# Strassen-Winograd output projections: the second product by halves in turn with the first two, and one weight sum by accumulating DMA

## The chip, the cores and the metric

The kernel runs on one core of one Trainium2 chip, in float32. The metric is the device time of one execution in microseconds (us). TensorE (PE) multiplies; PEld is its weight load, which runs beside the multiplication. VectorE (DVE), ScalarE (ACT) and GpSimd (POOL) do the rest; SyncE (SP) and POOL issue DMA transfers between HBM and the on-chip memory (SBUF). TensorE writes into PSUM, of which this kernel uses eight banks.

## The reference

One layer of a decoder trunk with 512 tokens and 1024 channels (cut to what matters here):

```python
def reference(x, mem, ...):
    h = rmsnorm(x, norm_mix_g)
    proj = h @ w_in                                  # three branches and their gates
    up = einsum('bsnw,nwd->bsnd', branches, w_branch)
    merged = sum(sigmoid(gate_logits + b_gate) * up, axis=2)
    x = x + merged @ w_o                             # output projection 1
    h = rmsnorm(x, norm_xa_g)
    mem_n = rmsnorm(mem, norm_mem_g)
    x = x + memory_attention(h, mem_n, w_xq, w_xkv, w_xo)   # ends with o @ w_xo: projection 2
    h = rmsnorm(x, norm_mlp_g)
    x = x + square(relu(h @ w_up)) @ w_down
    return rmsnorm(x, final_g)
```

The two projections `merged @ w_o` and `o @ w_xo` are 512 x 1024 by 1024 x 1024 each; the sum with `x` is normalized right behind each of them.

## The kernel before, in words

**Precision.** Every float32 operand is split into a high and a low half (`fp32r`), and a product is three matmuls: high by high, high by low, low by high. For weights this is `parts_of` (lines 104 to 114): ACT casts the high half out of the raw block (line 112), VectorE subtracts it from the raw block (line 113). Both halves go into `w_part` buffers; there are ten (`WBUFS`), so five blocks are in flight. Raw blocks (`w_raw`, 128 x 1024, 512 KB) have six buffers (`RAWS`) and are loaded by SP in the order of a `Stream` (line 241).

**Seven products.** The projections with `w_o`, `w_xo` and `w_down` go by Strassen and Winograd: `items_w` (line 410). The 512 tokens are two halves of 256 (rows of A), the output channels two halves of 512 (columns of B), and seven products P1 to P7 take the place of eight. `LEFT` (line 405) names the left operand of each; these are made by `Pairs` (lines 376 to 403) for two blocks of 128 channels at a time, into `pr` tiles, and A12, which only P2 reads, into `pr_b`. The right operands are B11 (P1), B21 (P2), B22 (P3) and sums of blocks (P4 to P7). `TO` (line 407) says where each product's bank is added: P1 and P2 to the left 512 columns of tokens 0 to 255, P6 and P3 to the right columns of these, P5 and P7 to the right columns of tokens 256 to 511, P4 to their left ones. P1, P6, P7 and P4 accumulate in the two banks p1, P5 and P3 in the two banks p3, both from the pool `at`; P2 has two banks p2 from the pool `mm`, which has four and serves the ordinary projections. The add into `x` reads a bank in the middle of its use, so P6 waits for the adds of P1, and P3 for those of P5.

**Halves.** The inner dimension of a product comes in two halves, j = 0 and 1, each a raw block for each of B11, B12, B22 and B21: eight blocks of a set, in the load order B11 (j = 0), B12 (0), B11 (1), B12 (1), B22 (0), B22 (1), B21 (0), B21 (1). One half of a product is 12 matmuls of 128 x 512 (line 430). `ORDER` (line 177) is the order in which the halves are written: P1 and P5 by halves in turn, then P6, P3, P2, P7, P4 with both halves together.

**Weight sums.** Class `Wide` makes the sums on VectorE in place in the raw blocks (lines 191 to 200, `plus` in line 131): B11 + B12 for P5, two sums for P6, B11 + B21 for P4, each for both halves: eight sums of a set. `w_o` and `w_down` use it. Class `Summed` (lines 202 to 221), for `w_xo`, makes the same sums by accumulating DMAs from HBM that POOL issues (line 213).

**Norms.** `proj_norm` (line 1035) hangs work on the ends of the products: after P3 it loads the gain through POOL and begins the norm of tokens 0 to 255 with the sum of squares over the right columns (`norm_begin`, line 494); after P2 `norm_end` (line 503) takes the left columns, the power on POOL (line 480) and the scaled `xn`; after P7 it begins tokens 256 to 511 and transposes the first tile; after P4 it ends those. Beside the first projection the norm of the memory is made (`mem_norm`) and transposed after P6 and P3 through banks of the pool `at` into `mT_h` and `mT_l`, which the projection of the keys reads right after P4. Between the first and second item of the second projection stand the last two heads of the attention (`last_heads`, line 1166), whose results are left operands of the second halves.

**What sets the order.** The code calls the steps in the order of a list (`plan`, `run_plan` in line 266), and `Stream.pump` makes the weights' parts two steps ahead. That is not yet the order on the chip: the context of line 1369 plans the instructions of every engine with its own model of their durations, takes from what is ready the earliest of the list, and gives out buffers and banks as they come free. Each engine's order is then fixed in the program, and an engine waits for the instruction at its head.

Of the kernel before, what the change touches and what calls it, by code (L numbers as in the profile page):

```python
# [38 lines left out]
def trunk_kernel(ctx: ExitStack, tc: tile.TileContext, x, mem, par, rot, dqd, kdec, g_mix, g_xa, g_mem, g_mlp,  # L39
# [64 lines left out]
    def parts_of(src):  # L104
        n = src.shape[1]
        part = lambda: wpool.tile([P, CW], F32R, name="w_part", bufs=WBUFS)
        if 2 * n <= CW:
            both = part()
            wh, wl = both[:, :n], both[:, n:2 * n]
        else:  # L110
            wh, wl = part(), part()
        act.copy(out=wh, in_=src)  # L112
        dve.tensor_tensor(out=wl, in0=src, in1=wh.bitcast(F32), op=ALU.subtract)  # L113
        return wh, wl
# [28 lines left out]
    class Seven:  # L143
# [27 lines left out]
        def get(self):  # L171
            where = dict(B11=(0, 0), T1=(1, 0), T3=(1, 1), T2=(2, 0), T4=(2, 1), B22=(3, 0), B21=(3, 1))
            return {n: [w[:, o * 512:(o + 1) * 512].rearrange("p (a b) -> p a b", a=4) for w in self.parts[i]]
                    for n, (i, o) in where.items()}


    ORDER = [(p, j) for pair in (("P1", "P5"), ("P6",), ("P3",), ("P2",), ("P7",), ("P4",)) for j in (0, 1) for p in pair]

    class Wide:

        def __init__(self, t, c):
            self.t, self.c = t, c
            self.loads = [(t, c + i) for i in range(8)]
            at = dict(P1=0, P5=1, P6=4, P3=4, P2=6, P7=6, P4=6)
            self.need = [at[p] + (2 * j if at[p] < 4 else j) + 1 for p, j in ORDER]
            self.steps = [lambda raw, p=p, j=j: self.step(raw, p, j) for p, j in ORDER]
            self.parts = []

        def step(self, raw, p, j):
            b11, b12, b22, b21 = (raw[i] if i < len(raw) else None for i in (2 * j, 2 * j + 1, 4 + j, 6 + j))
            if p == "P5":
                plus(b11, b11, b12)
            elif p == "P6":
                plus(b11, b11, b22)
                plus(b12, b12, b22)
            elif p == "P4":
                plus(b11, b11, b21)
            return parts_of(dict(P3=b22, P2=b21, P7=b12).get(p, b11))  # L200

    class Summed(Wide):


        def __init__(self, t, c):
            super().__init__(t, c)
            self.need = [n + (n in (1, 3)) for n in self.need]

        def step(self, raw, p, j):
            b11, b12, b22, b21 = (raw[i] if i < len(raw) else None for i in (2 * j, 2 * j + 1, 4 + j, 6 + j))  # L210

            def acc(dst, i):
                pool.dma_start(out=dst, in_=self.t[self.c + i], accum_op=ALU.add)

            parts = parts_of(dict(P3=b22, P2=b21, P7=b12).get(p, b11))
            if p == "P1":
                acc(b11, 2 * j + 1)
                acc(b12, 4 + j)
            elif p in ("P5", "P6"):
                acc(b11, 4 + j if p == "P5" else 6 + j)  # L220
            return parts

    class Stream:
# [186 lines left out]
    def items_w(src, c, pairs, after=lambda p: None, kind=Wide):  # L410


        acc = {}

        def part(p, js, n):
            bank = dict(P2="p2", P5="p3", P3="p3").get(p, "p1")

            def fn(ws):
                ws = [wv(w, 2) for w in ws]
                if p in ("P1", "P5", "P2") and js[0] == 0:  # L420
                    for i in range(2):
                        acc[bank, i] = (mmps if p == "P2" else atps)(bank)

                def mm(i, j):
                    tok = slice(i * P, (i + 1) * P)
                    for k in range(2):
                        ah, al = [x[:, tok] for x in pairs(2 * j + k)[LEFT[p]]]
                        wh, wl = [w[:, k, :] for w in ws[j - js[0]]]
                        for m, (x, y) in enumerate(((ah, wh), (ah, wl), (al, wh))):
                            te.matmul(acc[bank, i], x, y, start=p in ("P1", "P5", "P2") and j + k + m == 0,  # L430
                                      stop=j == 1 and k == 1 and m == 2, skip_group_check=True)

                def add(i):
                    t, h, op = TO[p]
                    dst = S["x"][t + i][:, h * 512:(h + 1) * 512]
                    op(dst, dst, acc[bank, i])


                rows = p in ("P7", "P4")
                for i, j in [(i, j) for i in range(2) for j in js] if rows else [(i, j) for j in js for i in range(2)]:  # L440
                    mm(i, j)
                    if j == 1:
                        add(i)
            item(fn, (kind, src, c, n, n + len(js)))

        for n, (p, j) in enumerate(ORDER):
            if p in ("P1", "P5"):
                part(p, [j], n)
            elif j == 0:
                part(p, [0, 1], n)  # L450
            if j == 1:
                after(p)
# [41 lines left out]
    def norm_begin(key, src, c=0):  # L494

        S["xn", key] = unit("xn", (P, D), F32)
        S["ss", key] = small.tile([P, 2], F32, name="ss", bufs=6)
        ss = S["ss", key]
        sumsq(src, c, ss, 0, S["xn", key])
        dve.tensor_scalar(out=ss[:, 0:1], in0=ss[:, 0:1], scalar1=1.0 / D, scalar2=EPS,  # L500
                          op0=ALU.mult, op1=ALU.add)
# [21 lines left out]
    S = {}  # L523
# [508 lines left out]
    def reload_x():  # L1032
        S["x"] = load_x()

    def proj_norm(src, name, g, beside, after, first=lambda its: None, kind=Wide):


        def ends(p):
            if p == "P3":
                def begin():  # L1040
                    S["g"] = load_g(g, pool)
                    S["hT"] = Split("hT", KT)
                    for t in (0, 1):
                        norm_begin(t, S["x"][t], 1)
                item(begin)
            if p == "P2":
                item(lambda: [norm_end(t, S["x"][t], S["g"], 0) for t in (0, 1)])
            if p == "P7":
                item(lambda: [norm_begin(t, S["x"][t], 1) for t in (2, 3)])
                item(lambda: norm_T(0, S["hT"], 0))  # L1050
            if p == "P4":
                item(lambda: [norm_end(t, S["x"][t], S["g"], 0) for t in (2, 3)])
                item(lambda: norm_T(1, S["hT"], 1))
            beside(p)

        its = capture(lambda: items_w(src, 0, lambda k: S[name, k // 2].w[k % 2], ends, kind))
        first(its)
        plan.extend(its)
        after(lambda t: item(lambda: norm_T(t, S["hT"], t)))
# [313 lines left out]
```

## Time and profile before

| | before |
|---|---|
| runs, median (lowest to highest) | 1019.96 us (1017.85 to 1020.46), 3 runs |
| the profiled execution | 1020.44 us, its span 1018.7 us |
| mean granted clock of TensorE | 0.995 |
| TensorE busy | 994.7 us, 98% |
| VectorE busy | 717.3 us, 70% |
| ACT busy | 527.3 us, 52% |
| product with `w_o` in the trace | from 469.97 us to about 514.9 us |
| product with `w_xo` in the trace | from 627.67 us to about 677.35 us |

Times in the trace are us from the start of the span. A row of the timeline gives start, length, engine, line, operation, tiles and count; in brackets stands how long the engine was idle before it and what ended that. A row of TensorE that covers several matmuls runs from the first's start to the last's end; matmuls overlap, so the distance of their starts is less than their length.

### The profile page before, as it was taken

The page shows a single profiled execution, that of the slowest core. Times are in us where ns is not written, and L with a number is a line of the kernel's source. Part 1 is how long each engine was busy: PE and PEld are TensorE (multiplying, and loading weights), DVE is VectorE, ACT ScalarE, POOL GpSimd, SP SyncE. Part 2 cuts the span into 40 slices and gives each one's busy share as a digit, 9 for nine tenths or more (in the row PEclk, how much of TensorE's full clock was granted, in tenths as well). Part 3 has the DMA queues.
Part 4 walks back from the last instruction along what each step waited for, and adds up shares of the span by engine and source line. Part 5 has one row for each costly group of instructions (what it writes and reads, how often), then busy time and mean ns, then how long its engine had stood idle before and what let it go on. Part 6 is the DMA issues. An engine that isn't in the chain of part 4 may idle for free. (4 is left out here: it accounts for less than half of the span.)

```text
span 1018.7 us, 13121 instructions
## 1 busy us (share of the span) xinstructions
PE 994.7 (98%) x4958; PEld 840.6 (83%) x4958; DVE 717.3 (70%) x1063; ACT 527.3 (52%) x909; POOL 73.7 (7%) x133
## 2 busy tenths in 40 slices
PE   7999999999999999999999999999999999999996
PEld 5888888878888889987898888789888888888885
DVE  5657777777463787779895456875785786696785
ACT  6456666766432344444474445655553553553543
POOL 1000111223110000001110001000000000000001
PEclk9999999999999999999999999999999999999999
DMA  9242222222122212344554335642034125215212
GB/s 366 109 145 83 83 84 104 84 82 83 62 97 74 79 57 93 120 140 143 171 165 167 104 83 93 177 144 84 21 129 160 42 88 172 71 44 187 80 42 83
DMA packets 31600, 112.04 MB, mean 110 GB/s; under 512 B 3888, under 2 KB 3888, under 8 KB 31536
## 3 DMA queue, kind: packets, MB, share of 16 engines
q1 hardware_dynamic: 27648, 99.63, 28.3%
q0 software_dynamic: 2592, 9.44, 3.9%
q10 hardware_dynamic: 1296, 2.13, 0.6%
q8 instruction: 39, 0.64, 0.2%
q14 instruction: 25, 0.20, 0.1%
HBM read 109.08 MB, written 2.10 MB: 109 GB/s over the span
## 5 line engine op out<-in xcount | busy, mean ns | idle before, releaser
L113 DVE TENSOR_TENSOR w_part<-w_raw,w_part 128x1024 fp32r<-128x1024 f32 (+1 forms) x224 | 271.6, 1213 | 165.0 <-ACT w_part L112 158.4
L112 ACT CAST w_part<-w_raw 128x1024 fp32r<-128x1024 f32 (+1 forms) x224 | 233.4, 1044 | 287.3 <-PE mm L299 129.6
L299 PE MATMUL mm<-hT_l,w_part 128*128 128x512 f32 (+1 forms) x736 | 281.8, 383 | 1.7 <-DVE hT_l L288 1.7
L300 PE MATMUL mm<-hT_h,w_part 128*128 128x512 f32 (+1 forms) x736 | 281.6, 383 | 0.0
L298 PE MATMUL mm<-hT_h,w_part 128*128 128x512 f32 (+1 forms) x736 | 280.5, 384 | 1.1 <-DVE r_qk L795 1.1
L430 PE MATMUL p<-w_part,pr 128*128 128x512 f32 x864 | 203.1, 391 | 1.8 <-ACT pr L287 0.8
L430 PEld LDWEIGHTS p<-w_part,pr 128*128 128x128 f32 x864 | 161.7, 188 | 37.3 <-DVE x L131 1.4
L299 PEld LDWEIGHTS mm<-hT_l,w_part 128*128 128x128 f32 x736 | 139.4, 189 | 26.9 <-DVE hT_l L288 1.9
L300 PEld LDWEIGHTS mm<-hT_h,w_part 128*128 128x128 f32 x736 | 139.4, 189 | 25.6
L298 PEld LDWEIGHTS mm<-hT_h,w_part 128*128 128x128 f32 x736 | 138.3, 189 | 27.0 <-DVE r_qk L795 1.8
L131 DVE TENSOR_TENSOR w_raw<-w_raw 128x1024 f32<-128x1024 f32 (+1 forms) x48 | 54.3, 1131 | 0.7 <-DMA w_raw<-in_w_down_dram 0.3
L128 DVE TENSOR_TENSOR x<-x,p 128x512 f32<-128x512 f32 x48 | 32.6, 683 | 9.5 <-PE p L430 9.5
L430 PE MATMUL p<-w_part,pr_b 128*128 128x512 f32 x144 | 35.7, 401 | 2.7 <-DVE w_part L113 1.4
L430 PEld LDWEIGHTS p<-w_part,pr_b 128*128 128x128 f32 x144 | 27.6, 193 | 9.4 <-DVE w_part L113 1.8
L686 DVE TENSOR_TENSOR_SCAN sb_suf<-ones,sb_e 128x128 f32<-128x128 f32 (+3 forms) x32 | 27.5, 858 | 9.6 <-POOL sb_e L665 8.3
L298 PE MATMUL mm<-w_part,xg_h 128*128 128x512 f32 x64 | 26.4, 413 | 7.6 <-ACT xg_h L292 7.6
L131 DVE TENSOR_TENSOR x<-x,p 128x512 f32<-128x512 f32 x36 | 24.1, 682 | 11.5 <-PE p L430 11.4
L689 ACT ACTIVATE sb_suf<-sb_suf 128x128 f32<-128x128 f32 (+3 forms) x32 | 15.1, 471 | 29.7 <-DVE sb_suf L688 29.5
L299 PE MATMUL mm<-w_part,xg_h 128*128 128x512 f32 x64 | 25.8, 404 | 0.0
L356 PE MATMUL p<-mix_h,w_part 128*128 128x256 f32 x128 | 25.0, 283 | 0.0
L300 PE MATMUL mm<-w_part,xg_l 128*128 128x512 f32 x64 | 24.3, 389 | 0.0
L486 ACT ACTIVATE xn<-x 128x512 f32<-128x512 f32 x24 | 15.1, 629 | 15.8 <-DVE x L131 8.0
(239 smaller groups left out, 1434.2 us busy)
## 6 DMA issues: line engine op xcount, KB each, us to landing
w_raw<-in_w_in_dram SPq DMA_DIRECT2D x56, 512.0 KB, 3.3
w_raw<-in_w_up_dram SPq DMA_DIRECT2D x32, 512.0 KB, 3.8
w_raw<-in_w_down_dram SPq DMA_DIRECT2D x32, 512.0 KB, 3.3
w_raw<-in_w_br_dram SPq DMA_DIRECT2D x12, 512.0 KB, 3.4
w_raw<-in_w_gate_dram SPq DMA_DIRECT2D x8, 512.0 KB, 3.3
w_raw<-in_w_o_dram SPq DMA_DIRECT2D x8, 512.0 KB, 3.3
w_raw<-in_w_xk_dram SPq DMA_DIRECT2D x8, 512.0 KB, 3.3
w_raw<-in_w_xv_dram SPq DMA_DIRECT2D x8, 512.0 KB, 3.3
```

Source lines behind the costliest of these rows:

```text
L112: act.copy(out=wh, in_=src)
L113: dve.tensor_tensor(out=wl, in0=src, in1=wh.bitcast(F32), op=ALU.subtract)
L128: dve.tensor_tensor(out=out, in0=a, in1=b, op=ALU.subtract)
L131: dve.tensor_tensor(out=out, in0=a, in1=b, op=ALU.add)
L298: te.matmul(ps, lh, rh, start=first, stop=False)
L299: te.matmul(ps, lh, rl, start=False, stop=False)
L300: te.matmul(ps, ll, rh, start=False, stop=last)
L356: te.matmul(ps[:, :256], x[:, k, :], y, start=first and k == 0 and i == 0, stop=k == 3 and i == 2, skip_group_check=True)
L430: te.matmul(acc[bank, i], x, y, start=p in ("P1", "P5", "P2") and j + k + m == 0, stop=j == 1 and k == 1 and m == 2, skip_group_check=True)
L486: act.activation(out=dst[:, cs], in_=src[:, cs], func=AF.Square, accum_out=ss[:, i:i + 1])
L686: dve.tensor_tensor_scan(out=suf[:, :s][:, ::-1], data0=ones[:, :s], data1=e1[:, :s][:, ::-1], initial=0.0, op0=ALU.mult, op1=ALU.add)
L689: act.activation(out=suf[:, :s], in_=suf[:, :s], func=AF.Exp)
```

## The change

For `w_o` the new class `Early` takes the place of `Wide`, and `Summed` (for `w_xo`) is now built on `Early`. `w_down` keeps `Wide` and its order.

- P2 joins P1 and P5: the order is P1, P2, P5 (j = 0), P1, P2, P5 (j = 1), then P6, P3, P7, P4.
- The load order of a set is B11 (0), B21 (0), B12 (0), B11 (1), B21 (1), B12 (1), B22 (0), B22 (1).
- B21 is no longer in a raw buffer when P4's sum is due, so in `Early` that sum is an accumulating DMA onto B11, issued by POOL behind the split for P6. The other six sums stay on VectorE. In `Summed` the accumulation onto B12 is issued behind P2's split instead of P1's.
- The norm of tokens 0 to 255 begins after P6, with the left columns, and ends after P3 with the right ones.

```diff
-    ORDER = [(p, j) for pair in (("P1", "P5"), ("P6",), ("P3",), ("P2",), ("P7",), ("P4",)) for j in (0, 1) for p in pair]
+    def order(*groups):
+        return [(p, j) for g in groups for j in (0, 1) for p in g]
 
     class Wide:
+        TURN = ("P1", "P5")
+        ORDER = order(TURN, ("P6",), ("P3",), ("P2",), ("P7",), ("P4",))
+        LOADS = range(8)
+        NEED = dict(P1=0, P5=1, P6=4, P3=4, P2=6, P7=6, P4=6)
...
+        def add(self, dst, i):
+            pool.dma_start(out=dst, in_=self.t[self.c + i], accum_op=ALU.add)
...
+    class Early(Wide):
+        TURN = ("P1", "P2", "P5")
+        ORDER = order(TURN, ("P6",), ("P3",), ("P7",), ("P4",))
+        LOADS = (0, 6, 1, 2, 7, 3, 4, 5)
+        NEED = dict(P1=0, P2=6, P5=1, P6=4, P3=4, P7=4, P4=4)
 
         def step(self, raw, p, j):
+            b11, b12, b22, b21 = self.blocks(raw, j)
+            if p == "P5":
+                plus(b11, b11, b12)
+            elif p == "P6":
+                plus(b11, b11, b22)
+                plus(b12, b12, b22)
+            parts = parts_of(dict(P3=b22, P2=b21, P7=b12).get(p, b11))
+            if p == "P6":
+                self.add(b11, 6 + j)
+            return parts
+
+    class Summed(Early):
+        NEED = dict(Early.NEED, P2=1)
+
+        def step(self, raw, p, j):
+            b11, b12, b22, b21 = self.blocks(raw, j)
             parts = parts_of(dict(P3=b22, P2=b21, P7=b12).get(p, b11))
             if p == "P1":
-                acc(b11, 2 * j + 1)
-                acc(b12, 4 + j)
+                self.add(b11, 2 * j + 1)
+            elif p == "P2":
+                self.add(b12, 4 + j)
             elif p in ("P5", "P6"):
-                acc(b11, 4 + j if p == "P5" else 6 + j)
+                self.add(b11, 4 + j if p == "P5" else 6 + j)
             return parts
...
-        for n, (p, j) in enumerate(ORDER):
-            if p in ("P1", "P5"):
+        for n, (p, j) in enumerate(kind.ORDER):
+            if p in kind.TURN:
                 part(p, [j], n)
             elif j == 0:
                 part(p, [0, 1], n)
...
-    def proj_norm(src, name, g, beside, after, first=lambda its: None, kind=Wide):
+    def proj_norm(src, name, g, beside, after, first=lambda its: None, kind=Early):
         def ends(p):
-            if p == "P3":
+            if p == "P6":
                 def begin():
                     S["g"] = load_g(g, pool)
                     S["hT"] = Split("hT", KT)
                     for t in (0, 1):
-                        norm_begin(t, S["x"][t], 1)
+                        norm_begin(t, S["x"][t])
                 item(begin)
-            if p == "P2":
-                item(lambda: [norm_end(t, S["x"][t], S["g"], 0) for t in (0, 1)])
+            if p == "P3":
+                item(lambda: [norm_end(t, S["x"][t], S["g"]) for t in (0, 1)])
```

More of the change, by code (lines that the diff above doesn't have):

```diff
@@ L174, in get, with blocks @@
                     for n, (i, o) in where.items()}
-    ORDER = [(p, j) for pair in (("P1", "P5"), ("P6",), ("P3",), ("P2",), ("P7",), ("P4",)) for j in (0, 1) for p in pair]
+    def order(*groups):
+        return [(p, j) for g in groups for j in (0, 1) for p in g]
     class Wide:
+        TURN = ("P1", "P5")
+        ORDER = order(TURN, ("P6",), ("P3",), ("P2",), ("P7",), ("P4",))
+        LOADS = range(8)
+        NEED = dict(P1=0, P5=1, P6=4, P3=4, P2=6, P7=6, P4=6)
         def __init__(self, t, c):
             self.t, self.c = t, c
[L185 to L188, printed above, removed]
+            self.loads = [(t, c + i) for i in self.LOADS]
+            self.need = [self.LOADS.index((2 * j if i < 4 else j) + i) + 1 for i, j in
+                         ((self.NEED[p], j) for p, j in self.ORDER)]
+            self.steps = [lambda raw, p=p, j=j: self.step(raw, p, j) for p, j in self.ORDER]
             self.parts = []
+        def blocks(self, raw, j):
+            at = [self.LOADS.index(i) for i in (2 * j, 2 * j + 1, 4 + j, 6 + j)]
+            return [raw[i] if i < len(raw) else None for i in at]
+        def add(self, dst, i):
+            pool.dma_start(out=dst, in_=self.t[self.c + i], accum_op=ALU.add)
         def step(self, raw, p, j):
-            b11, b12, b22, b21 = (raw[i] if i < len(raw) else None for i in (2 * j, 2 * j + 1, 4 + j, 6 + j))
+            b11, b12, b22, b21 = self.blocks(raw, j)
             if p == "P5":
@@ L200, in step @@
             return parts_of(dict(P3=b22, P2=b21, P7=b12).get(p, b11))
[L202 to L207, printed above, removed]
-        def step(self, raw, p, j):
-            b11, b12, b22, b21 = (raw[i] if i < len(raw) else None for i in (2 * j, 2 * j + 1, 4 + j, 6 + j))
-            def acc(dst, i):
-                pool.dma_start(out=dst, in_=self.t[self.c + i], accum_op=ALU.add)
+    class Early(Wide):
[3 more added lines that the diff above has]
+        NEED = dict(P1=0, P2=6, P5=1, P6=4, P3=4, P7=4, P4=4)
+        def step(self, raw, p, j):
+            b11, b12, b22, b21 = self.blocks(raw, j)
[11 more added lines that the diff above has]
+        def step(self, raw, p, j):
+            b11, b12, b22, b21 = self.blocks(raw, j)
             parts = parts_of(dict(P3=b22, P2=b21, P7=b12).get(p, b11))
             if p == "P1":
-                acc(b11, 2 * j + 1)
-                acc(b12, 4 + j)
+                self.add(b11, 2 * j + 1)
+            elif p == "P2":
+                self.add(b12, 4 + j)
             elif p in ("P5", "P6"):
-                acc(b11, 4 + j if p == "P5" else 6 + j)
+                self.add(b11, 4 + j if p == "P5" else 6 + j)
             return parts
```

## The prediction

> **What bounds the kernel now.** I read the page first, then the waits of TensorE, then the timeline of TensorE through the two products that the change touches, then stretches with their granted clock, then the queues that feed them.
>
> ```profile
> PE 994.7 (98%) x4958; PEld 840.6 (83%) x4958; DVE 717.3 (70%) x1063; ACT 527.3 (52%) x909; POOL 73.7 (7%) x133
> ```
>
> TensorE is busy for 994.7 of 1018.7 us, and the edit adds or removes no matmul. Only the 24 us outside can be gained, and matmul time at a reduced clock. The waits of TensorE say where they are (columns: total us, times, longest):
>
> ```profile
> PE mm L298 <- ACT xg_h L292: 7.6, 1, 7.6
> PE mm L299 <- DVE hT_l L288: 1.7, 1, 1.7
> PE p L430 <- DVE w_part L113: 1.4, 1, 1.4
> PE p L430 <- ACT w_part L112: 1.4, 1, 1.4
> ...
> PE p L430 <- ACT pr L287: 0.8, 1, 0.8
> PE p L430 <- DVE x L131: 0.5, 1, 0.5
> PE p L430 <- DVE pr L288: 0.4, 1, 0.4
> ```
>
> The 7.6 us are the first load. Nearly all others lie in the two products with L430 that are to be reordered, or at their end (`hT_l`). `w_down`, which the edit leaves as it was, has none. First the product with `w_o`:
>
> ```profile
> 469.97 11.04 PE L430 MATMUL p<-w_part,pr 128*128 128x512 f32 x48
> 482.38 0.73 PE L430 MATMUL p<-w_part,pr_b 128*128 128x512 f32 x2 [1.36 <-ACT w_part L112]
> 484.48 3.87 PE L430 MATMUL p<-w_part,pr_b 128*128 128x512 f32 x10 [1.37 <-DVE w_part L113]
> 488.14 11.41 PE L430 MATMUL p<-w_part,pr 128*128 128x512 f32 x48
> ```
>
> A half of one of the seven products is 12 matmuls. The 48 take 11.04 us, of which 0.39 is the last one's length, so one starts every (11.04 - 0.39) / 47 = 0.2266 us and a half takes 2.72 us. The first 48 are P1 and P5 by halves. Next comes `pr_b`, which is A12, and only P2 reads it: the planner already places the first half of P2 ahead of P6 and P3, although the code has P2 after both. Those 12 should fill 480.85 (469.97 + 48 x 0.2266) to 483.57; P6 starts at 488.14. Lost: 4.57 us. The two waits are only part of that:
>
> ```profile
> 480.80:488.10 7.30, 4.57 (x13) 3.14 (x13) 7.17 (x9) 1.20 (x3) 0.00 (x0) 0.82 0.44 144
> 641.80:647.20 5.40, 3.71 (x13) 2.02 (x12) 5.31 (x11) 3.98 (x7) 0.00 (x0) 1.00 0.63 186
> 679.80:683.40 3.60, 3.59 (x17) 3.59 (x18) 3.21 (x8) 1.07 (x3) 0.54 (x1) 0.53 0.66 220
> 486.00:489.00 3.00, 3.00 (x9) 2.38 (x8) 1.98 (x4) 1.04 (x1) 0.00 (x0) 0.52 0.36 145
> ```
>
> (Stretch, length, busy us of PE, PEld, DVE, ACT and POOL with counts, then the granted clock, DMA share, GB/s.) After the waits the clock was 0.52 from 486 to 489: the ten matmuls from 484.48 to 488.14 took 3.66 us instead of 2.27, 1.39 of the 4.57.
>
> Why was P2 waiting? Its block of weights was the seventh to be loaded, and its first transfer started when the 48 matmuls were almost over:
>
> ```profile
> 478.02 3.89 SPq L241 DMA_DIRECT2D w_raw<-in_w_o_dram  x2
> 481.28 1.04 ACT L112 CAST w_part<-w_raw 128x1024 fp32r<-128x1024 f32 x1 [0.47 <-DMA w_raw<-in_w_o_dram]
> 482.07 1.22 DVE L131 TENSOR_TENSOR w_raw<-w_raw 128x1024 f32<-128x1024 f32 x1
> 483.20 1.22 DVE L113 TENSOR_TENSOR w_part<-w_raw,w_part 128x1024 fp32r<-128x1024 f32 x1
> 484.34 0.68 DVE L131 TENSOR_TENSOR x<-x,p 128x512 f32<-128x512 f32 x1
> 484.95 1.23 DVE L131 TENSOR_TENSOR w_raw<-w_raw 128x1024 f32<-128x1024 f32 x1
> ```
>
> Only six raw buffers exist and eight blocks are wanted, so the seventh waits for a buffer. The sums on `w_raw` at 482.07 and 484.95 are B11 + B21 for P4, 20 us before P4 needs them; the first stands ahead of P2's low half (483.20). The add of P1 into `x` (484.34), for which P6 must wait since both use bank p1, stands behind.
>
> Now the product with `w_xo`, and what follows it:
>
> ```profile
> 637.68 4.26 PE L430 MATMUL p<-w_part,pr 128*128 128x512 f32 x18
> 642.79 2.83 PE L430 MATMUL p<-w_part,pr 128*128 128x512 f32 x10 [0.85 <-ACT pr L287]
> 646.04 0.73 PE L430 MATMUL p<-w_part,pr 128*128 128x512 f32 x2 [0.42 <-DVE pr L288]
> 647.24 11.22 PE L430 MATMUL p<-w_part,pr 128*128 128x512 f32 x48 [0.47 <-DVE x L131]
> 677.35 0.71 PE L298 MATMUL mm<-hT_h,w_part 128*128 128x256 f32 x4
> 679.81 0.44 PE L299 MATMUL mm<-hT_l,w_part 128*128 128x256 f32 x1 [1.75 <-DVE hT_l L288]
> ```
>
> The 18 end their turn at 637.68 + 18 x 0.2266 = 641.76; the next 12 are due 2.72 us and P6 starts at 647.24: 5.48 - 2.72 = 2.76 us lost, waiting for the left operands of the last attention heads (`pr`) and for one add. Here the clock stayed at 1.00. The wait for `hT_l` costs 679.81 - 677.83 = 1.98 us (the four short matmuls before it start 0.12 us apart: (0.71 - 0.36) / 3, 0.36 being the length of one, in the row at 516.74 below) and after it 17 that took 3.6 us at clock 0.53 instead of 2.04: 3.5 us in all.
>
> **The change, part by part.**
>
> *P2 by halves behind P1, `w_o`.* Its block moves from seventh to second in the load order. The first three `w_o` loads were issued here:
>
> ```profile
> 426.94 12.46 SPq L241 DMA_DIRECT2D w_raw<-in_w_o_dram  x3
> 469.94 1.06 ACT L112 CAST w_part<-w_raw 128x1024 fp32r<-128x1024 f32 x1 [0.53 <-PE mm L299]
> 472.66 1.06 ACT L112 CAST w_part<-w_raw 128x1024 fp32r<-128x1024 f32 x1 [1.66 <-PE p L430]
> ```
>
> The second is out by 439.4, 30 us before the product, so the late transfer is gone. What is late next? B22 is now seventh and waits for P2's block to be split. Splitting is paced by ten `w_part` buffers, two a half, so a half's cast comes when the half five places earlier is through on TensorE: 469.94 is the fifth cast, 472.66 the sixth, after P1's first 12. The fifth half is now P2's second: cast 1.06 and subtraction 1.22 end by 472.3, the load takes 3.3 (below), two sums 2.44; P6's second half is eighth, cast at 478.1, ready at 480.4. It is used at 469.97 + 84 x 0.2266 = 489.0. Cover: 8.6 us.
>
> P6 also needs both adds of P1. In before the first ended at 485.02, 6.9 us after P1's last matmul (469.97 + 36 x 0.2266 = 478.13). Now 24 matmuls, 5.44 us, lie between. Unchanged, the lag would cost 1.45 (with a clock drop 1.39 more); ahead of that add stood one sum and the late block's split, 2.44 us, which are gone or early. So 0 to 2.84; I take 0. Term: **-4.57 us**.
>
> *P4's sum by accumulating DMA, `w_o`.* Two VectorE sums of 1.22 us go; two DMA issues come on POOL's queue, and 1 MB more is read. `w_xo` already has eight such:
>
> ```profile
> L213 POOL DMA_DIRECT2D w_raw<-in_w_xo_dram x8: 866/872/973, 575.5 to 638.6; - x8
> DMA to landing us min/median/max: 3.1/3.3/10.2
> w_raw<-in_w_xo_dram POOLq DMA_DIRECT2D x8, 512.0 KB, 5.2
> 495.95 1.53 POOL L480 TENSOR_TENSOR rstd<-ms,half 128x1 f32<-128x1 f32 x1 [29.29 <-DVE ms L490]
> 499.02 0.56 POOL L480 TENSOR_TENSOR rstd<-ms,half 128x1 f32<-128x1 f32 x1 [1.53 <-DVE ms L490]
> ```
>
> P6's second half is split by 480.4, so the later sum is issued by 481.3 and lands 5.2 later, at worst 10.2: 491.5. P4 starts at 469.97 + 144 x 0.2266 = 502.6. Hidden by 11 us, and POOL sat idle for 29.29 us there. Term 0, if nothing stands ahead on POOL.
>
> *Norm begun from the left.* Two of four sums of squares on ACT and the load of the gain move ahead of P3; the other two stay between P3 and P7. ACT is busy 52%, and the matmuls of P3 lie over it. Term 0.
>
> *End of the `w_o` product.* Between P3 and the keys' projection stood P2's second half, P7 and P4; now only P7 and P4. In that time the memory's norm is transposed through the banks that P3 frees, and split:
>
> ```profile
> 516.19 0.68 DVE L288 TENSOR_TENSOR mT_l<-at,mT_h 128x512 fp32r<-128x512 f32 x1
> 516.36 0.63 PE L517 MATMUL at<-ident,xn 128*128 128x128 f32 x4 [0.38 <-DVE ss L500]
> 516.74 0.36 PE L299 MATMUL mm<-mT_l,w_part 128*128 128x256 f32 x1
> 503.45 1.28 DVE L131 TENSOR_TENSOR x<-x,p 128x512 f32<-128x512 f32 x2
> ```
>
> The last `mT_l` was ready at 516.87 and its reader started at 516.74 (another quarter): nothing to spare. The cover shrinks by 2.72 us. Out of VectorE's way go P2's two adds, 1.28 us, which now come before P6. So 2.72 - 1.28 = 1.44 us late. Bounds: 0, if the two sums of squares moved ahead help as well, and 2.72 + 1.39 = 4.1 with no relief and a clock drop. I take 1.44, the difference of two rows. Term: **+1.44 us**.
>
> *`w_xo`.* All four sums were by DMA and stay so; only the order changes. P2's first half (heads 0 and 1, ready) and the part of its second that reads head 2, 18 matmuls or 4.1 us, can now run while head 3 is prepared; the hole was 2.76. P1's adds get 5.44 us before P6 too. P2's block is second of eight to load here too. Between nothing and all of it; since 4.1 exceeds 2.76, I take all: **-2.76 us**. The wait for `hT_l` comes after P7 and P4 as before: 0, between -3.5 and +2.76 (below).
>
> Sum: -4.57 - 2.76 + 1.44 = -5.89. The profiled execution took 1020.44 us for its span of 1018.7: 1014.55. The median of the runs, 1019.96, is 0.48 lower: **1014.1 us**.
>
> **A rule of the skill on the clock.** The row: two waits of 1.4 us with two matmuls between them brought 0.52. The Trainium skill, "TensorE: Matmul & The Clock Gate", section "What's actually happening", says that the clock halves after about 3.4 us of idle in a free-running window. Read as a whole idle window, these waits would cause no drop and the gain in `w_o` would be 3.18, so 1015.5; the trace has the drop, so the measurement decides. No run here yet shows from what length on.
>
> **Rivals.**
>
> *The time comes back at the ends (1019.5 us).* The holes were time in which VectorE caught up: it was busy for 7.17 of 7.30 and 5.31 of 5.40 us in them. Then 4.1 of the 4.57 returns at the keys' projection, and 2.76 at `hT_l`: 1020.44 - 0.47, less 0.48. For it: both ends have no slack now. Against it: two sums leave VectorE in `w_o`, and what it waits for is itself TensorE's progress (the casts above).
>
> *`w_xo` gains nothing (1016.8 us).* P2's two banks come from the four that heads 2 and 3 use; if it gets none, or its parts are late, the hole stays: -4.57 + 1.44. Against it: those heads' banks are copied out before the hole.
>
> *The wait for `hT_l` goes too (1009.1 us).* -7.33 - 3.5 in all, with no loss at the keys. For it: work moves ahead of P3. Against it: what stands just ahead of `hT_l` is the split of `w_up`, which isn't touched.
>
> *Slower (1023.1 us): POOL's queue.* If the planner puts the accumulating DMAs behind the memory norm's powers, they go out from 499.6, the second at 500.5, and with the longest landing P4's weights are there at 500.5 + 10.2 + 1.06 + 1.22 = 513.0, against 502.6 + 1.36: 9.0 us late, 1.39 for the clock: -7.33 + 10.4 = +3.1, the cover for `mT` being given by the wait. It decides once the issue is later than about 495. The 29.29 idle us speak against it. The Trainium skill, "SBUF — State Buffer", section "SBUF: two separate sides", adds that VectorE in a two-port mode can keep GpSimd from writing descriptors; no run here shows it.
>
> *It doesn't do what it says:* the planner had P2 ahead of P6 already; if it now puts P2 elsewhere, this is the first rival.
>
> **How the numbers follow.** Forecast 0.42; time comes back 0.24; `w_xo` nothing 0.15; `hT_l` too 0.11; slower 0.08. About 0.3% (3 us) is what a measurement here can tell. 1016.8 lies at that line, so half of it counts as faster: 0.42 + 0.11 + 0.08 = 0.61; same 0.24 + 0.07 = 0.31; slower 0.08. The range 1010.5 to 1020.5 holds the forecast with its bounds, the second rival and most of the first, and leaves out the last and most of the third.
>
> **What would show it.** Right: no wait of L430 for `w_part` in `w_o`, clock 1.00 up to P4, `pr_b` in two groups of 12 within the first 72, no wait for `pr` in `w_xo`. The handover: TensorE waiting for `mT` by 1 to 2 us. Wrong: L430 waiting for `w_raw` sums of P6, a POOL issue after 495, or a longer wait for `hT_l`.

## The result: 0.27% slower, and the profile after

The changed kernel takes 1021.97 us (median of 9 runs, 1019.89 to 1022.92), the kernel before 1018.82 us on the same chip (9 runs, 1017.85 to 1020.46). The ratio is 1.0027, with a 95% interval from 1.0019 to 1.0036: slower, and by 3.15 us in the medians, where 1014.1 us and a gain of 5.9 had been forecast. The profiled execution took 1022.67 us for a span of 1021.0; that of before had a span of 1018.7. Of all runs of this document one is left out of the ratios, one of e12's five, which took 1874.23 us at a mean clock of 0.825.

The busy times of the engines in the changed kernel, and then the waits of TensorE (L457 is now the line of the seven products' matmuls, L544 that of the transposes, L325 to L327 those of the ordinary projections; columns of the waits: total us, times, longest):

```profile
PE 994.7 (97%) x4958; PEld 841.6 (82%) x4958; DVE 715.0 (70%) x1061; ACT 527.6 (52%) x909; POOL 75.8 (7%) x135
```

```profile
PE p L457 <- DVE x L131: 2.9, 1, 2.9
PE at L544 <- DVE x L131: 2.0, 1, 2.0
PE at L544 <- DVE mT_l L315: 1.1, 1, 1.1
...
PE mm L325 <- ACT mT_h L314: 1.0, 1, 1.0
PE at L544 <- DVE hT_l L315: 0.8, 1, 0.8
PE mm L326 <- DVE hT_l L315: 0.7, 1, 0.7
PE mm L325 <- ACT hT_h L314: 0.6, 1, 0.6
```

The waits that were to go are gone: none of L457 for `w_part`, none for `pr`. New ones stand in their place: 2.9 us for `x`, and 4.1 us at the handover to the keys (`x` at the transposes, `mT_l`, `mT_h`). The timeline of TensorE shows where; first the product with `w_o`, then the first score of the memory attention, then the end of the product with `w_xo`:

```profile
471.09 2.88 PE L457 MATMUL p<-w_part,pr 128*128 128x512 f32 x12
...
484.69 2.88 PE L457 MATMUL p<-w_part,pr 128*128 128x512 f32 x12
490.51 18.23 PE L457 MATMUL p<-w_part,pr 128*128 128x512 f32 x72 [2.94 <-DVE x L131]
...
516.49 0.74 PE L325 MATMUL mm<-mT_h,w_part 128*128 128x256 f32 x4 [0.95 <-ACT mT_h L314]
520.09 0.66 PE L544 MATMUL at<-ident,xn 128*128 128x128 f32 x4 [1.99 <-DVE x L131]
521.82 1.12 PE L544 MATMUL at<-ident,xn 128*128 128x128 f32 x4 [1.08 <-DVE mT_l L315]
...
575.71 0.28 PE L325 MATMUL xsc<-xk_h,xq_h 128*128 128x256 f32 x1
...
653.65 19.21 PE L457 MATMUL p<-w_part,pr 128*128 128x512 f32 x84
...
680.71 0.74 PE L325 MATMUL mm<-hT_h,w_part 128*128 128x256 f32 x4 [0.63 <-ACT hT_h L314]
682.65 0.63 PE L544 MATMUL at<-ident,xn 128*128 128x128 f32 x4 [0.76 <-DVE hT_l L315]
684.02 0.38 PE L326 MATMUL mm<-hT_l,w_part 128*128 128x256 f32 x1 [0.74 <-DVE hT_l L315]
```

Two marks split both kernels in the same way: the first matmul of P1 in `w_o`, and the first score. In the kernel before the score came at:

```profile
569.20 0.28 PE L298 MATMUL xsc<-xk_h,xq_h 128*128 128x256 f32 x1
```

- From P1 to the first score: 569.20 - 469.97 = 99.2 us before, 575.71 - 471.09 = 104.6 after: **5.4 us lost**.
- From the score to the end of the span: 1018.7 - 569.20 = 449.5 before, 1021.0 - 575.71 = 445.3 after: **4.2 us gained**, by `w_xo`.
- Ahead of P1 1.1 us more, in work that the edit doesn't touch. In the other kernels below P1 starts between 470.10 and 471.46, so I take this for scatter between executions.

So one half of the change works, and `w_o` takes back more than that. Why `x` was late is told by POOL's timeline, first before, then after (the bracket gives how long POOL had been idle and what ended that):

```profile
441.31 0.76 POOL L100 DMA_DIRECT2D x<-in_x_dram  x1 [96.11 <-PE mm L299]
455.89 0.55 POOL L100 DMA_DIRECT2D x<-in_x_dram  x1 [13.82 <-DVE pr L288]
463.40 1.07 POOL L100 DMA_DIRECT2D x<-in_x_dram  x2 [6.97 <-PE mm L300]
```

```profile
481.76 1.05 POOL L203 DMA_DIRECT2D w_raw<-in_w_o_dram  x1 [135.43 <-DVE w_part L113]
482.54 2.43 POOL L100 DMA_DIRECT2D x<-in_x_dram  x4
484.69 0.79 POOL L94 DMA_DIRECT2D g_bc<-in_g_mem_dram  x1
485.22 1.31 POOL L1026 DMA_DIRECT2D m_sb<-in_mem_dram  x2
487.73 0.89 POOL L203 DMA_DIRECT2D w_raw<-in_w_o_dram  x1 [1.20 <-DVE w_part L113]
```

`x` isn't kept on the chip and is loaded again for the residual sum (L100). Before, each of these loads went out, by its bracket, as soon as the last reader of its buffer was done: 441.3, 455.9, 463.4. Now the first accumulating DMA (L203) stands ahead of all four, and of the memory's gain and rows. It waits for the split of P6's weights (`w_part`, L113), and everything behind it on POOL waits too: the idle time of 135 us before it covers all the time in which the loads used to go. They are issued 20 to 41 us later, all at once, beside the weights. Landing takes longer as well (columns: size, median us from issue to landing; first before, then after):

```profile
x<-in_x_dram POOLq DMA_DIRECT2D x4, 512.0 KB, 3.9
m_sb<-in_mem_dram POOLq DMA_DIRECT2D x2, 512.0 KB, 8.1
```

```profile
x<-in_x_dram POOLq DMA_DIRECT2D x4, 512.0 KB, 9.4
w_raw<-in_w_o_dram POOLq DMA_DIRECT2D x2, 512.0 KB, 11.2
m_sb<-in_mem_dram POOLq DMA_DIRECT2D x2, 512.0 KB, 15.2
```

The add of P1 onto `x` waited for that load (VectorE), P6 for the add, and the sums of squares of the memory's norm (ACT) for `m_sb`. From the timelines of VectorE and ACT, and then two stretches with the clock that followed (columns as in the prediction):

```profile
489.77 1.41 DVE L131 TENSOR_TENSOR x<-x,p 128x512 f32<-128x512 f32 x2 [2.80 <-DMA x<-in_x_dram]
...
499.99 0.63 ACT L513 ACTIVATE xn<-m_sb 128x512 f32<-128x512 f32 x1 [1.27 <-DMA m_sb<-in_mem_dram]
```

```profile
490.40:495.00 4.60, 4.49 (x13) 3.56 (x14) 3.16 (x5) 0.00 (x0) 0.45 (x1) 0.63 1.02 411
515.00:525.00 10.00, 5.98 (x36) 5.26 (x35) 9.90 (x17) 4.56 (x11) 1.99 (x2) 0.84 0.63 209
```

The account of `w_o` closes. Before, 4.57 us were lost ahead of P6, 0.37 in the low clock behind it (48 matmuls in 11.41 instead of 11.04) and 0.38 at the keys; without these the stretch would be 99.2 - 5.3 = 93.9. After, P6 was due at 471.09 + 72 x 0.2266 = 487.41 and came 3.1 late; its 72 matmuls took 18.23 instead of 16.48, 1.75 for the clock; the keys waited 0.95 + 1.99 + 1.08 = 4.0 and about 1.6 went to the second low stretch (10 us at 0.84). Together 10.5, and 93.9 + 10.5 = 104.4, against 104.6 measured.

### The profile page after: what moved, and what is told of

It is laid out like the page before. It is cut to its first block, busy times and chain, and to the rows that moved or that the text cites. A ratio compares the mean times of both kernels' runs of the same rounds, so it can differ in the third digit from the quotient of the medians.

```text
span 1021.0 us, 13129 instructions
## 1 busy us (share of the span) xinstructions
PE 994.7 (97%) x4958; PEld 841.6 (82%) x4958; DVE 715.0 (70%) x1061; ACT 527.6 (52%) x909; POOL 75.8 (7%) x135
## 4 chain that ended last, share of the span: by engine, by line
PE 92%; DVE 3%; issue 1%; DMA 1%; ACT 1%; POOL 0%; DVEq 0%; POOLq 0%; SPq 0%
PE mm L326 21%; PE mm L325 21%; PE mm L327 21%; PE p L457 19%; PE p L383 4%; DVE w_part L113 1%; PE o L759 1%; PE aT L725 1%; DMA x<-in_x_dram 1%; PE z L701 0%; DMA w_raw<-in_w_in_dram 0%; PE z L702 0%; DVE x L131 0%; PE at L544 0%; PE xsc L327 0%
## 5 line engine op out<-in xcount | busy, mean ns | idle before, releaser
L113 DVE TENSOR_TENSOR w_part<-w_raw,w_part 128x1024 fp32r<-128x1024 f32 (+1 forms) x224 | 271.5, 1213 | 162.4 <-ACT w_part L112 155.9
L325 PE MATMUL mm<-hT_h,w_part 128*128 128x512 f32 (+1 forms) x736 | 280.1, 383 | 1.7 <-DVE r_qk L822 1.1
L327 PE MATMUL mm<-hT_h,w_part 128*128 128x512 f32 (+1 forms) x736 | 280.6, 382 | 0.0
L457 PE MATMUL p<-w_part,pr 128*128 128x512 f32 x864 | 202.8, 392 | 3.0 <-DVE x L131 2.9
L457 PEld LDWEIGHTS p<-w_part,pr 128*128 128x128 f32 x864 | 162.9, 189 | 37.9 <-DVE x L131 3.9
L325 PEld LDWEIGHTS mm<-hT_h,w_part 128*128 128x128 f32 x736 | 137.7, 188 | 27.9 <-DVE r_qk L822 1.8
L327 PEld LDWEIGHTS mm<-hT_h,w_part 128*128 128x128 f32 x736 | 138.5, 188 | 25.7
L131 DVE TENSOR_TENSOR w_raw<-w_raw 128x1024 f32<-128x1024 f32 (+1 forms) x46 | 51.8, 1127 | 0.6 <-DMA w_raw<-in_w_o_dram 0.3
L457 PE MATMUL p<-w_part,pr_b 128*128 128x512 f32 x144 | 34.8, 389 | 0.0
L325 PE MATMUL mm<-w_part,xg_h 128*128 128x512 f32 x64 | 26.7, 417 | 7.8 <-ACT xg_h L319 7.8
L457 PEld LDWEIGHTS p<-w_part,pr_b 128*128 128x128 f32 x144 | 27.0, 188 | 5.6
L327 PE MATMUL mm<-w_part,xg_l 128*128 128x512 f32 x64 | 24.6, 395 | 0.0
```

The source lines that it names most:

```text
L131: dve.tensor_tensor(out=out, in0=a, in1=b, op=ALU.add)
L325: te.matmul(ps, lh, rh, start=first, stop=False)
L327: te.matmul(ps, ll, rh, start=False, stop=last)
```

## The experiments

All are compared with the kernel before on the same chip. "P1 to score" and "score to end" are the two stretches above in the profiled execution. The kernel before was run again beside each set, and each ratio goes by these runs: median 1019.85 us beside e1 to e4 (one chip), 1018.99 beside e5 to e8 and 1019.85 beside e9 to e12 (another chip). Medians of different sets are therefore compared by their ratios.

| kernel | `w_o` | `w_xo` | median us | ratio, 95% interval | P1 to score | score to end |
|---|---|---|---|---|---|---|
| before | old order, sums on VectorE | old | 1018.82 | | 99.2 | 449.5 |
| after | new order, DMA sum first on POOL | new | 1021.97 | 1.0027 (1.0019 to 1.0036) | 104.6 | 445.3 |
| e1 | new order, B21 loaded again | new | 1015.63 | 0.9957 (0.9939 to 0.9976) | 97.5 | 445.2 |
| e2 | as after, `x` and memory loaded by ACT | new | 1023.35 | 1.0029 (1.0015 to 1.0043) | 106.6 | 444.9 |
| e3 | old | new | 1015.86 | 0.9958 (0.9937 to 0.9978) | 97.6 | 445.3 |
| e4 | as after | old | 1025.33 | 1.0045 (1.0030 to 1.0060) | 105.2 | 449.0 |
| e5 | new order, DMA sum behind `x` | new | 1017.24 | 0.9980 (0.9971 to 0.9989) | 100.2 | 445.2 |
| e6 | as e5, P3 ahead of P6 | new | 1016.47 | 0.9964 (0.9951 to 0.9976) | 96.8 | 445.2 |
| e7 | as e5, half of P2 kept late | new | 1012.74 | 0.9935 (0.9923 to 0.9948) | 95.0 | 445.2 |
| e8 | as e1, norm begun after P3 | new | 1014.45 | 0.9953 (0.9939 to 0.9966) | 96.9 | 445.1 |
| e9 | order of e7, B21 loaded again | new | 1014.02 | 0.9931 (0.9910 to 0.9952) | 94.9 | 446.1 |
| e10 | the kernel of e1 | new | 1016.35 | 0.9961 (0.9945 to 0.9977) | 97.5 | 445.2 |
| e11 | the kernel of e5 | new | 1017.32 | 0.9969 (0.9957 to 0.9981) | 100.3 | 445.3 |
| e12 | the kernel of e7 | new | 1012.50 | 0.9917 (0.9897 to 0.9937) | 95.0 | 445.3 |

### The two projections apart: e3 and e4

e3 gives `w_o` its old class, order and norm and leaves `w_xo` changed; e4 does the reverse.

```diff
-    proj_norm(w_o, "mp", g_xa, mem_beside, kv_proj)
+    proj_norm(w_o, "mp", g_xa, mem_beside, kv_proj, kind=Wide)      # e3, with the old norm for Wide
...
-    proj_norm(w_xo, "xo", g_mlp, lambda p: None, first_up, last_heads, Summed)
+    proj_norm(w_xo, "xo", g_mlp, lambda p: None, first_up, last_heads, Summed0)   # e4: old Summed, old norm
```

> Only w_xo gets the new order; w_o keeps the old one, its norm too. By the two traces the stretch from the first score to the first long run of w_down went from 168.9 to 164.7 us, so both theories expect before minus 4.2 us, about 1014.6. If the gain there is only time lost earlier and caught up, 1017 to 1019.

> Only w_o gets the new order (with accumulating DMA and norm); w_xo keeps the old one. Both theories: stretch from P1 to the first score 104 to 105 us as in the changed kernel, from there on 168 to 169 as before, so before plus 5.4 us, about 1024. If the two projections depend on each other, less than 1022.

`w_xo` alone gains: 0.9958. From the score to the end all kernels with the new `w_xo` but e9 take 444.9 to 445.3 us, the two with the old one 449.5 and 449.0. `w_o` alone loses: 1.0045, with P6 waiting 3.5 us for `x`. By these stretches the two halves of the change don't touch each other, and it is the loss of `w_o` that needs an explanation. e3 and the kernel before have the same `w_o`, yet 97.6 and 99.2 us from P1 to the score; most of this is a low clock that only one of the two executions had (the last section).

### Is it the accumulating DMA? e1

The order and the norm stay new. The two blocks of B21 are loaded a second time by SP, as ninth and tenth, and P4's sum is made on VectorE; no accumulating DMA is left in `w_o`.

```diff
+    class Again(Early):
+        LOADS = (0, 6, 1, 2, 7, 3, 4, 5, 8, 9)        # 8 and 9 read blocks 6 and 7 once more
+        NEED = dict(Early.NEED, P4=8)
...
+            elif p == "P4":
+                plus(b11, b11, raw[8 + j])
```

> P4's sum for w_o is made on VectorE again, with B21 loaded a second time by SP; the accumulating DMA leaves POOL's queue, the order of the products and of the norm stays changed. Queue theory (the loss in w_o comes from x and the memory being loaded by POOL behind an accumulating DMA that waits for P6's split): P6's wait of 2.94 us goes, and the waits at the keys' projection (0.95, 1.99, 1.08) shrink to 1.5 or less; from the start of P1 to the first attention score about 96 to 100 us instead of 104.6, time 1014 to 1017. Order theory (P2 by halves leaves too little cover before P6 and before the keys): P6 still waits 1.5 to 3 us, the stretch stays above 103 us, time 1020 to 1022.

The loss is gone: 0.9957, with the same bytes read. TensorE in e1:

```profile
483.87 19.58 PE L477 MATMUL p<-w_part,pr 128*128 128x512 f32 x84
...
511.20 0.73 PE L345 MATMUL mm<-mT_h,w_part 128*128 128x256 f32 x4 [0.52 <-ACT mT_h L334]
513.59 0.66 PE L564 MATMUL at<-ident,xn 128*128 128x128 f32 x4 [1.20 <-DVE x L131]
515.33 0.66 PE L564 MATMUL at<-ident,xn 128*128 128x128 f32 x4 [1.08 <-DVE mT_l L335]
```

and a stretch ahead of the keys:

```profile
500.00:515.00 15.00, 12.53 (x68) 10.14 (x66) 15.00 (x22) 10.51 (x20) 2.79 (x2) 1.00 0.50 169
```

P1 started at 470.27, so the 61st matmul came 13.60 us later, which is 60 x 0.2266: nothing is lost ahead of P6, and L477 waits for nothing up to the end of P4. But the keys wait 0.52 + 1.20 + 1.08 = 2.8 us, while VectorE is busy for the whole of the 15 us from 500 on (15.00). e1 and e3 differ by 0.2 us in the median: with `x` in time and the sum on VectorE, the new order of `w_o` gains nothing over the old one.

### Does another queue help? e2

The accumulating DMAs stay; the loads of `x`, of the memory and of its gain go to ACT's queue.

```diff
-            pool.dma_start(out=xs[t], in_=x[t * P:(t + 1) * P, :])
+            act.dma_start(out=xs[t], in_=x[t * P:(t + 1) * P, :])
```

> The changed kernel with its accumulating DMA as it is, but x, the memory and its gain are loaded from ACT's queue instead of POOL's. Queue theory: x and the memory come before the adds need them, P6's wait goes, the stretch from P1 to the first score 96 to 100 us, time 1014 to 1017. Order theory: as the changed kernel, 1020 to 1022, stretch above 103 us. If the transfers themselves collide (DMA share 0.97 to 1.02 from 486 to 495 us), something between, with the loads landing late though they are issued early.

It doesn't: 1.0029. In e2 `x` is issued at 481.8 as well, this time behind the casts of the weights, and P6 waits in two parts:

```profile
481.18 1.05 ACT L112 CAST w_part<-w_raw 128x1024 fp32r<-128x1024 f32 x1 [1.44 <-PE p L457]
481.82 0.33 ACTq L100 DMA_DIRECT2D x<-in_x_dram  x1
...
487.84 3.02 PE L457 MATMUL p<-w_part,pr 128*128 128x512 f32 x12 [0.81 <-DVE x L131]
493.00 15.53 PE L457 MATMUL p<-w_part,pr 128*128 128x512 f32 x60 [2.14 <-DVE x L131]
```

This corrects the theory. POOL as such isn't the fault. The code calls the loads of `x` ahead of the projection, but in e2 the planned order of ACT has them behind casts of its weights, and in the changed kernel that of POOL has them behind the first accumulating DMA. On ACT each cast waits for TensorE to give back a buffer (1.44 us for the one shown). That the plan has these loads as late in the kernel before too, and that they were early there only because nothing ahead of them on POOL had to wait, fits e2 and e5; no trace shows it.

### The same DMA, behind `x`: e5

Only the place is changed: the two accumulating DMAs of `w_o` are tied to stand behind the last load of the memory in POOL's order.

```diff
-            if p == "P6":
-                self.add(b11, 6 + j)
+            if p == "P6":
+                with tc.issue_after(S["m_last"].ins):     # S["m_last"]: the last load of the memory
+                    self.add(b11, 6 + j)
```

> The changed kernel with one thing different: in the projection with w_o the two accumulating DMAs are tied to stand behind the loads of x and of the memory in POOL's order. Bytes, queues and work stay the same. Queue-head theory (the accumulating DMA, put first on POOL, made its own wait the wait of the loads of x, which in the kernel before ran some 40 us ahead of their place in the plan): x is out by 465 us, no wait of L457 for x, P1 to P6 13.6 us, time as with the sum on VectorE, 1014 to 1016.5 us. Traffic theory (the accumulating DMAs cost the time wherever they are issued, since 1 MB more is moved and they land late): P6 still starts late or P4 waits for its weights, 1019 us or more.

The ratio is 0.9980 (0.9969 as e11). POOL and TensorE in e5:

```profile
464.17 1.06 POOL L100 DMA_DIRECT2D x<-in_x_dram  x2 [6.96 <-PE mm L328]
...
481.96 0.90 POOL L203 DMA_DIRECT2D w_raw<-in_w_o_dram  x1 [14.53 <-DVE w_part L113]
...
484.34 19.60 PE L458 MATMUL p<-w_part,pr 128*128 128x512 f32 x84
...
511.69 0.74 PE L326 MATMUL mm<-mT_h,w_part 128*128 128x256 f32 x4 [0.95 <-ACT mT_h L315]
513.57 0.66 PE L545 MATMUL at<-ident,xn 128*128 128x128 f32 x4 [0.70 <-DVE x L131]
515.30 0.66 PE L545 MATMUL at<-ident,xn 128*128 128x128 f32 x4 [1.08 <-DVE x L131]
517.04 0.66 PE L545 MATMUL at<-ident,xn 128*128 128x128 f32 x4 [1.08 <-DVE mT_l L316]
```

The accumulating DMA is issued at the same time as in the changed kernel (481.96 against 481.76) and moves the same bytes, but `x` is out before it: no wait of P6, and P1 to P6's place 484.34 - 470.74 = 13.60 us. That the DMA made `x` late by its place in the queue, and not by its traffic, is shown by this run. The time is 0.7 us over the 1014 to 1016.5 expected, for the keys wait longer here than in e1: 3.8 us, and a low clock behind it, 0.63 from 517 to 520 and 0.80 from 520 to 523. In e11, the same kernel, this low clock lasted longer:

```profile
513.50:520.00 6.50, 5.03 (x23) 4.23 (x23) 6.19 (x11) 2.25 (x8) 1.05 (x2) 0.50 0.83 238
```

So from P1 to the score this kernel takes 1.0 us more than the one before, though nothing is late ahead of P6. Between 509 us and the last `mT_l` VectorE makes four splits of weights (L113) in e5 and two in e1; ahead of 497.17 it had stood idle for 2.70 us in e5. Why the plan put these splits later isn't shown.

### The handover to the keys: e6 and e7

Both stand on e5. e6 puts P3 ahead of P6, so that P3's banks, through which the memory is transposed, come free 5.4 us earlier; the norm then begins after P3 and ends after P6. e7 keeps the order of before, with only the block of P2's first half loaded early; P2's second half stays behind P3, and the norm begins from the right columns.

```diff
+    class Third(Early):                                   # e6
+        TURN = ("P1", "P5", "P2")
+        ORDER = order(TURN, ("P3",), ("P6",), ("P7",), ("P4",))
+        LOADS = (0, 1, 6, 2, 3, 7, 4, 5)
...
+    class Kept(Early):                                    # e7
+        TURN = ("P1", "P5", "P2")
+        ORDER = (order(("P1", "P5")) + [("P2", 0)] + order(("P6",), ("P3",)) + [("P2", 1)] +
+                 order(("P7",), ("P4",)))
+        LOADS = (0, 1, 2, 3, 6, 4, 5, 7)
```

> As the run before (accumulating DMAs behind the loads of x and the memory), and in the projection with w_o the order is P1, P5, P2 by halves, then P3 ahead of P6. P3 frees its two banks one product (5.4 us) earlier, so the memory's norm can be transposed earlier. Cover theory (the waits of 2.8 us at the keys' projection are the 2.72 us of cover that P2's second half had given): they go, 1.5 to 3 us less than the run before. Rival: VectorE, busy for all of the 15 us ahead, is what is late there, and P3 waits for the adds of P5, with only 12 matmuls between: no gain or up to 2 us more.

> As the first run of this set, but in the projection with w_o only the first half of P2 goes ahead of P6, behind P1 and P5, and its second half stays behind P3, as in the kernel before; its first block is loaded fifth, and the norm begins from the right columns as before. Cover theory: P1 to P6 13.6 us as with the new order (no wait for weights), and the handover to the keys without waits over 0.5 us as in the kernel before: 2 to 3 us less than the first run, 1011.5 to 1013.5 us. Rival (VectorE's work is only put off, and whatever is saved ahead of P6 comes back at the keys): within 1 us of the first run.

In e6 the waits for `mT` go, as the cover theory said, but P7 waits 2.1 us for the adds of P6: 0.9964, some 0.8 us less than e5 in the median, where 1.5 to 3 us less had been expected of the cover theory. (Its five runs stand at two levels, two at 1014.2 and three at 1016.5 us; the profiled one is of the lower.) VectorE is busy for 14.3 of the 15 us from 500 here too, which speaks for the rival as well: what VectorE has to do late stays late. e7 is the fastest kernel of the study, 0.9935 and as e12 0.9917: some 6 to 7 us under before, while the changed kernel is 3 over it. Its TensorE:

```profile
483.70 11.04 PE L465 MATMUL p<-w_part,pr 128*128 128x512 f32 x48
...
512.21 0.66 PE L552 MATMUL at<-ident,xn 128*128 128x128 f32 x4 [1.08 <-DVE mT_l L323]
```

From P1 at 470.10 to P6 again 13.60 us: the hole of 4.57 is closed with one half of P2, and the other half is still there for the end. One wait of 1.08 is left at the keys, and 93.9 + 1.08 gives the 95.0 of the table. Against e5 the norm's columns are changed beside the order; the two weren't tried apart.

### The norm: e8

e1 with the norm of tokens 0 to 255 begun after P3 instead of P6 (still from the left columns).

```diff
-            if p == "P6":
+            if p == "P3":
                 def begin():
```

> The version with the second block loaded again and P4's sum on VectorE, with the norm of tokens 0 to 255 begun after P3 instead of P6 in both projections (still from the left columns, all else the same). Nothing theory (the earlier start of two sums of squares on ACT lies beside matmuls and ends no wait): within 1 us of that version, 1015 to 1016.5 us. Rival (it shortens the waits at the keys and at hT_l): 1 to 2 us more.

0.9953 against 0.9957 and 0.9961 of e1 and e10: the earlier beginning of the norm is worth nothing that can be measured.

### What the DMA costs where it is: e9 to e12

Four kernels side by side: the order of e7 and the new order, each with B21 loaded again and with the accumulating DMA behind `x`. e9 is e7 with the sums of e1; the others are e1, e5 and e7 once more.

> The order of e7 in the projection with w_o (P2's second half kept behind P3, norm from the right), with P4's sum on VectorE and the two blocks loaded again by SP in place of the accumulating DMAs. If the accumulating DMA, once it stands behind the loads of x, costs nothing itself: within 1 us of e7 (e12). If it costs (longer landing beside other transfers, or its transfers delay others): 1 to 2 us less than e12. If VectorE's two sums of 1.22 us matter more: 1 to 2 us more than e12.

> The kernel of e1 once more, beside the three others on one chip: new order in w_o, P4's sum on VectorE with the blocks loaded again. From e1 and e5: about 2 us less than e11. If the distance between e1 and e5 was that of two sets: within 1 us of e11.

> The kernel of e5 once more, beside the others: new order in w_o, accumulating DMAs behind the loads of x and the memory. From e5: 2 us less than before, with 3.8 us of waits at the keys.

> The kernel of e7 once more, beside the others: 6 us less than before, as in e7; 4 us less than e11.

In the order of e7 the accumulating DMA takes 1012.50 us against 1014.02 with the second load, in the new order 1017.32 against 1016.35: one each way, and the intervals of the ratios overlap. The second distance is half of the 2 us expected for e10. By the first alone VectorE's two sums would matter, the third expectation of e9; but from P1 to the score the profiled executions of e9 and e12 are equal, 94.9 and 95.0, and what e9 has more, 0.8 us, lies behind the score, where the two have the same code. The ratio of e7, the same kernel as e12, is no better than that of e9, 0.9935 against 0.9931. In the new order the four runs of e10 with the higher mean clock lie under all of e11, the other four among them. So in its right place the DMA costs nothing that shows; it also saves nothing certain. The order (with its norm) is worth more: e12 is 4.8 us under e11, e9 2.3 under e10.

## Why the prediction was wrong

**The step that failed** is "P4's sum by accumulating DMA, `w_o`": "Term 0, if nothing stands ahead on POOL". It asked only what the two DMAs would stand behind. It didn't ask what would stand behind them, though the page before showed the loads of `x` and of the memory on the same queue. The 29.29 us of idle POOL that it leaned on begin right behind these loads, the last of which was issued at 466.12. The order of POOL isn't the order of the code: the planner put the DMA first. The true size of the term is e5 against the changed kernel: 100.2 against 104.6 from P1 to the score, **4.4 us**. The issues themselves came at 481.76 and 487.73, the later one 6.4 us behind the 481.3 forecast; TensorE still didn't wait for P4's weights. The Trainium skill, "DMA: Bandwidth & Descriptors", section "Anatomy of one DMA — SWDGE (gpsimd) path", says that the DMA engines don't wait for semaphores and that any wait is held by the issuing sequencer; by that rule a DMA that waits holds its whole queue, and POOL's 135.43 us of idle time, with four loads issued right after it, agree.

**"P2 by halves behind P1, `w_o`", -4.57.** The mechanism was right: in e1, e5 and e7 the hole is closed to the last tenth (13.60 us for 60 matmuls), and the weights for P2 are no longer waited for in the changed kernel. The sub-step "P6 also needs both adds of P1 ... 0 to 2.84; I take 0" failed only where `x` came late, in the changed kernel by 2.94 us plus 1.75 for the clock (e2 and e4 alike), and for a reason that had not been named: not the lag of VectorE but the target of the add. Where `x` is there, 0 is right. Of the 4.57, 1.39 was a low clock that e3, with waits of nearly the same length, didn't have (below): its hole was 3.35 us.

**"End of the `w_o` product", +1.44, is a second step that failed, and about as large.** It was right in kind: at the keys TensorE waits for what P2's second half used to cover, and e7, which leaves that half late, keeps one wait of 1.08. Its size was wrong. The forecast's own kernel with `x` in time is e5: 100.2 - 93.9 = 6.3 us over the floor, against 0.4 before, so **+5.9**, outside the bounds 0 to 4.1; e11 gives the same. Of the 6.4 in e11 3.1 are waits and about 2.5 the low clock (5.03 us busy at 0.50); the rest, 0.8, isn't traced. With the sum on VectorE, in e1, it is 97.5 - 93.9 = 3.6, so +3.2: 2.8 of waits, no low clock, and 0.8 untraced. The credit of 1.28 for P2's two adds on VectorE doesn't show: from 500 on VectorE was busy for 15.00 of 15.00 us in e1 and in e5. For `w_o` -4.57 + 1.44 = -3.1 us had been forecast; without the late `x`, in e5, it is 100.2 - 99.2 = +1.0, and the late `x` makes it +5.4. So 4.1 of the 8.5 us between forecast and result would have been there with a free queue too. The first rival, "the time comes back at the ends", describes `w_o` once its DMA is moved: e1 is equal to e3, and e5 is not even that (0.9980 against 0.9958). e7 shows that this was a matter of how much of P2 is taken forward.

**"`w_xo`", -2.76.** The stretch gained 4.2. Up to the first matmul on `hT_h` it is (677.35 - 569.20) - (680.71 - 575.71) = 3.15, the hole of 2.76 and 0.4 more, which I didn't trace. The wait for `hT_l` was to stay, and nearly did: 0.76 + 0.74 in two pieces, where 1.75 had been. But the low clock behind it didn't come (3.6 us for 2.04 of work in the prediction's account), and behind that first matmul on `hT_h` the span is 1.1 us shorter. In e4, whose old `w_xo` had no low clock there either, the stretch is 449.0 us, so 3.7 of the 4.2 don't hang on it.

**The rivals.** "`w_xo` gains nothing" and "the wait for `hT_l` goes too" are out. "Slower: POOL's queue" named the right queue and came close in time (1023.1), but by another mechanism: it had the DMAs too late, behind the norm's powers. They went out at 481.8 and 487.7, before its bound of 495, and they harmed by what stood behind the first of them: e5 issues it at the same time without harm. That its time came close is luck. Of what was to show the prediction wrong, none happened; the sign was a wait for `x`, which hadn't been listed, and the clock, which wasn't 1.00 up to P4. The range ended at 1020.5 since that rival had been left out.

## What to carry to other kernels

When an operation becomes a DMA on a queue that waits, list what stands behind it on that queue, and see how long before its place in the program that work now runs: loads that are early only because nothing blocks their queue lose all of that lead at once. Tie the order of such a queue by hand, or keep loads and waiting DMAs apart. When work is pulled forward to fill a hole, look whether it was the cover of something later, and pull only as much as the hole takes.

## What the hardware showed that was not expected

**The low clock is a matter of chance for waits of this size.** Stretches of 3 to 3.6 us behind waits, one row each: before (two waits of 1.36 and 1.37), e3 (1.48 and 1.25), e4 (one of 1.75 for `hT_l`):

```profile
485.50:488.75 3.25, 3.25 (x9) 2.49 (x8) 2.48 (x4) 0.79 (x1) 0.00 (x0) 0.50 0.47 160
```

```profile
486.00:489.00 3.00, 3.00 (x15) 2.45 (x14) 2.98 (x5) 1.05 (x1) 0.00 (x0) 1.00 0.54 175
```

```profile
688.00:691.60 3.60, 3.42 (x29) 3.43 (x30) 3.37 (x9) 1.08 (x3) 0.55 (x1) 1.00 0.74 253
```

Two waits of nearly the same length brought 0.50 in one execution and 1.00 in another, and the 1.75 us for `hT_l`, which had brought 0.53 before, brought 1.00 in e4. Waits of 2.9 and 3.5 us (after and e4, for `x`) were both followed by it; of two of 2.1 us, the one in e2 was (0.59 from 493 to 496.5) and the one in e6 wasn't (1.00 from 503.8 to 507.3). Read in steps of 0.25 us, the clock stands at 0.50 for 13 or 14 steps running, 3.25 to 3.5 us, in the kernel before, the changed one, e4 and e5, and once each for 27 and 26 steps in e2 and e11. So one low stretch takes up to about 1.7 us of matmul time, an estimate from the 0.50 and these lengths. The runs show the chance too: of the eight of e10, one kernel, four had a mean clock of 0.998 and took 1014.3 to 1015.7 us, four had 0.995 and took 1017.0 to 1017.8. The Trainium skill, "TensorE: Matmul & The Clock Gate", section "What's actually happening", has a clock of half or full, by a window of about 3.4 us that runs freely; that agrees with the 0.50, the lengths and the chance. It has the drop after a whole idle window, and there the trace differs: before, 1.75 us for `hT_l` were enough. From what share of a window on isn't settled by these runs. A term that is read from one execution's low clock, like the 1.39 above, is thus paid by some runs only.

**Loads that go out together land later.** The same loads of `x` took 3.9 us to land when they were spread from 441 to 464 us, and 9.4 when they went out together beside the weights, with the DMA engines' share at 1.02 (490.4 to 495).
